# Copying gated tiles into planes of halves six products behind the gated product, with tiles of their own

## The chip, the core and the metric

The kernel runs on one core of a Trainium2 chip. Five engines work beside each other, each through its own queue of instructions in the order in which they were written: TensorE (PE, with PEld for the loading of weights), VectorE (DVE), ScalarE (ACT), GpSimd (POOL), and SyncE (SP), which here only issues DMAs. They wait for one another by semaphores. The metric is the device time of one execution in microseconds (us), lower being better, taken as the median of several runs. The profile is one execution recorded by the hardware profiler; its lines name engine, source line and tiles.

## The reference

A trunk of two layers over 256 tokens of width 1024, in float32. Each layer is a gated feed-forward stage, a mixer (attention) and another gated feed-forward stage, so there are four feed-forward stages, numbered 0, 2, 3 and 5 in the kernel (1 and 4 are the mixers):

```python
def swiglu(h, w_gate, w_up, w_down):
    return (jax.nn.silu(h @ w_gate) * (h @ w_up)) @ w_down

for layer in range(DEPTH):
    x = x + 0.5 * swiglu(rms_norm(x, ffn1_norm[layer]), ...)
    x = x + mixer(rms_norm(x, mix_norm[layer]))
    x = x + 0.5 * swiglu(rms_norm(x, ffn2_norm[layer]), ...)
return rms_norm(x, final_norm)
```

The hidden width of a feed-forward stage is 2816. The change touches only these stages: the product silu(gate) * up, called the gated product here, and its way to the down projection.

## The kernel before

**Split products.** Every float32 operand is split in two parts, hi (rounded to the format that PE takes) and lo (the rest). One product of a 128-deep slice is three matmuls (hi x hi, lo x hi, hi x lo; `mm`, lines 466 to 468). Weights come by DMA in tiles called raw (line 376, three buffers of up to 1 MB, issued by SP once a buffer is free), ACT makes hi (line 474) and DVE makes lo (line 477). Seven pairs of split tiles may be alive.

**Tokens and chunks.** The 256 tokens are two halves (tt = 0, 1) of 128 rows. A feed-forward stage runs over five chunks of 512 hidden columns and a mixed one of 256. A plain chunk takes gate for both halves (2 x 8 products), then up for both (2 x 8 products). Some chunks are done by a Strassen scheme instead (`seven_gates`), with 29 or 30 products and sums on DVE (lines 392 and 762 to 808). After the chunks come the down products, partly by Strassen pairs too, for which blocks of the gated tiles are summed (`quarters`, `sums_of`).

**The way of a gated tile.** ACT applies silu to the gate (line 667 or 785), DVE multiplies with up (`glu`, line 672, or line 789 in a Strassen chunk) and the result lies in a tile glu (ring of two). It must be transposed. This is done by DMA on 16-bit halves: ACT copies the tile into two planes, the low and the high halves (line 551), SP issues a DMA transpose of the planes back into the tile glu (line 553), and ACT copies the transposed halves together again into the tile of the planes (line 555). From there ACT and DVE make the parts g_h and g_l (lines 474 and 477), which the down products read. The tile of the planes has the tag silu, in a ring of three, shared with the results of silu and with the temporaries of the Strassen sums.

**What sets the order.** Each engine's queue has the order in which the program issues instructions. PE's order is written out by the loops. Everything else is done by generators (tasks): `mm` ends in `tick`, which counts one product and lets every task whose count has run out issue its next piece, and which also issues the next hi and lo parts when a rate says so. A `yield n` in a task puts its next piece n products later. So `GLU_WAIT` is the number of products between the issue of the gated product and that of the first copy, `TURN_WAIT[0]` that between the copy and the DMA transpose, and `TURN_WAIT[1]` that between the transpose and the second copy. These numbers set a place in the queues, not a time: an instruction waits in its queue until what it needs is there, and what stands behind it waits as well.

Of the kernel before, what the change touches and what calls it, by code (L numbers as in the profile page):

```python
# [18 lines left out]
P = 128  # L19
# [32 lines left out]

X_WAIT = 5
R_WAIT = 3
GLU_WAIT = 1
TURN_WAIT = [1, 8]
NAT_WAIT = 2
ROPE_WAIT = [3, 3]
KB_WAIT = {
# [143 lines left out]
class Trunk:  # L203
# [342 lines left out]

    def turned_over(self, m, w):

        two = self.t([P, 512], "silu", 3)
        planes, back = (t.bitcast(U16)[:, : 2 * w] for t in (two, m))  # L550
        self.nc.scalar.copy(planes.rearrange("p (h c) -> p h c", h=2), back.rearrange("p (c h) -> p h c", h=2))  # L551
        yield TURN_WAIT[0]
        self.nc.sync.dma_start_transpose(back.rearrange("p (j t) -> p j t", t=P), planes)
        yield TURN_WAIT[1]
        self.nc.scalar.copy(planes.rearrange("p (c h) -> p h c", h=2), back.rearrange("p (h c) -> p h c", h=2))  # L555
        yield 1
        return two
# [96 lines left out]
    def ffn(self):  # L654
# [96 lines left out]
        def seven_gates(f0, w, pairs7):  # L751

            while len(K) < 4:
                self.tick(False)
            self.rate = SEVEN_RATE[self.now.n]
            h, M, c = self.now.hT, {}, {}
            op = nc.vector.tensor_tensor

            def copy():
                yield 1  # L760
                c["m"] = self.t([P, 512], "glu", 2)
                nc.scalar.activation(c["m"], M["1"], AF.Copy)

            def common():

                yield 1
                while "m" not in c:
                    yield 1
                w = self.t([P, 512], "silu", 3)
                op(w, M["6"], c["m"], op=ALU.add)  # L770
                yield 1
                y = self.t([P, 512], "glu", 2)
                op(y, M["5"], w, op=ALU.subtract)
                yield 1
                nc.vector.scalar_tensor_tensor(w, M["7"], -1.0, w, op0=ALU.mult, op1=ALU.add)
                c["y"], c["w"] = y, w

            def first_gate():
                yield 1
                while "m" not in c:  # L780
                    yield 1
                s = self.t([P, 512], "silu", 3)
                op(s, M["00"], c["m"], op=ALU.add)
                yield 1
                nc.scalar.activation(s, s, AF.Silu, scale=self.now.r[0])
                c["s"] = s

            def up(tt, o, u, s):
                nc.vector.scalar_tensor_tensor(o, u, self.now.r[tt], s, op0=ALU.mult, op1=ALU.mult)
                self.spawn(transposed(tt, f0, w, o), GLU_WAIT)  # L790
                yield 1

            def rest():
                yield 1
                while "s" not in c or "w" not in c:
                    yield 1
                y, z, m = c["y"], c["w"], c["m"]
                op(y, M["01"], y, op=ALU.add)
                yield 1
                tasks.append(self.start(up(0, y, y, c["s"])))  # L800
                yield 1
                op(m, M["10"], z, op=ALU.add)
                yield 1
                nc.scalar.activation(m, m, AF.Silu, scale=self.now.r[1])
                op(z, M["5"], z, op=ALU.subtract)
                yield 1
                if "11" in M:
                    op(z, M["11"], z, op=ALU.add)
                    yield 1
                tasks.append(self.start(up(1, m, z, m)))  # L810

            def product(name, lh, piece, first, last):
                self.mm(M[name], lh, piece, first, last)

            n7 = KD // 2 - pairs7
            M.update((name, self.bank(tag)) for name, tag in [("00", "s"), ("01", "s"), ("10", "s")])
            if n7:
                M["11"] = self.bank("o")
            for q in range(KD // 2):
                k, first, last = 2 * q, q == n7, q == KD // 2 - 1  # L820
                if q < n7:
                    pieces = self.take(4)
                    for i in range(2):
                        for n, piece in enumerate(pieces[2 * i : 2 * i + 2]):
                            for tt in range(NT):
                                product(f"{tt}{n}", h[tt][k + i], piece, k + i == 0, tt == n == 1 and i == 1 and q + 1 == n7)
                    continue
                b11, b21, b22, t7, t5, t8, t6 = self.take(7)
                if first:
                    for task in tasks:  # L830
                        self.finish(task)
                    M.update((name, self.bank(tag)) for name, tag in [("1", "pj"), ("5", "pj"), ("7", "tp")])
                    M["6"] = self.bank("tp" if n7 else "o")
                j = q - (KD // 2 - most)
                product("1", h[0][k + 1], b11, first, last)
                if last:
                    self.start(copy())
                product("00", h[0][k], b21, q == 0, last)
                if last:
                    tasks.append(self.start(first_gate()))  # L840
                product("01", K[0][j], b22, q == 0, last)
                product("7", K[3][j], t7, first, last)
                product("5", K[2][j], t5, first, last)
                product("10", h[1][k], t8, q == 0, last)
                product("6", K[1][j], t6, first, last)
            self.start(common())
            tasks.append(self.start(rest()))

        f0 = 0
        self.spawn(x_sums())  # L850
        for ci, w in enumerate(FF_CHUNKS):
            if ci in sevens:
                seven_gates(f0, w, sevens[ci])
                f0 += w // P
                continue
            self.rate = (AHEAD_RATE if ci + 1 in sevens else RATE)[self.now.n]

            tags = ["pj", "s", "s", "pj"] if ci - 1 in sevens else ["s", "s", "pj", "pj"]
            G = self.take(KD)
            S = []  # L860
            if self.now.n + ci == 0:
                both = self.first_gates(G)
            for tt in range(NT):
                g = both[tt] if self.now.n + ci == 0 else self.project(self.ready(tt), G, tags[tt])
                S.append(self.t([P, 512], "silu", 3))
                self.start(silu(tt, w, g, S[tt]))
            U = self.take(KD)
            for tt in range(NT):
                u = self.project(self.now.hT[tt], U, tags[NT + tt])
                tasks.append(self.start(glu(tt, f0, w, u, S[tt])))  # L870
            f0 += w // P

        w, V = FF_MIXED, self.take(KD)
        for tt in range(NT):
            both = self.project(self.now.hT[tt], V, "s")
            s = self.t([P, 512], "silu", 3)
            self.start(silu(tt, w, both, s))
            tasks.append(self.start(glu(tt, f0, w, both[:, w:], s)))
        W = {}
# [46 lines left out]
        def combine():  # L926

            op = nc.vector.scalar_tensor_tensor
            x = lambda tt, i: self.x[tt][:, i * 512 : i * 512 + 512]
            more = lambda o, y: nc.vector.tensor_tensor(o, o, y, op=ALU.add)  # L930
            yield 1
            c = self.t([P, 512], "silu", 3)
            nc.scalar.activation(c, M["1"], AF.Copy, scale=0.5)
            op(x(0, 0), M["1"], 0.5, x(0, 0), op0=ALU.mult, op1=ALU.add)
            yield 1
            v = self.t([P, 512], "silu", 3)
            op(v, M["6"], 0.5, c, op0=ALU.mult, op1=ALU.add)
            yield 1
            w = self.t([P, 512], "glu", 2)
            op(w, M["7"], -0.5, v, op0=ALU.mult, op1=ALU.add)  # L940
            yield 1
            y = self.t([P, 512], "silu", 3)
            op(y, M["5"], 0.5, v, op0=ALU.mult, op1=ALU.subtract)
            yield 1
            more(x(0, 1), y)
            z = self.t([P, 512], "glu", 2)
            yield 1
            op(z, M["5"], 0.5, w, op0=ALU.mult, op1=ALU.subtract)
            yield 1
            more(x(1, 0), w)  # L950
            yield 1
            more(x(1, 1), z)
# [610 lines left out]
```

## Time and profile before

| | us |
|---|---|
| median of three runs | 1036.34 |
| the three runs | 1036.03, 1036.34, 1039.86 |
| the profiled execution | 1039.17 |
| its span, first to last instruction | 1037.4 |

The mean granted clock of TensorE over the span is 0.974 of full speed. A row of the page's second part shows it in 40 slices of the span (tenths of full speed, 9 being 90% or more):

```profile
PEclk9998999999999989999999998999999999999999
```

Rows of the timeline give the start and the length of an instruction in us, then engine, line, operation, tiles written and read, shapes, and in brackets how long the engine was idle before it and what it had waited for. Rows of the windows give a stretch, its length, the busy time of each engine in it with the number of its instructions, the granted clock, the DMA engines' share and GB/s. Rows of the waits give who waited for whom: us in total, times, and the longest.

### The profile page before, as it was taken

The numbers are of one execution on the slowest core, as the hardware profiler recorded it, in microseconds if no ns is written. First come the engines' busy times: TensorE is split into PE (matmuls) and PEld (weight loads), VectorE is DVE, ScalarE is ACT, GpSimd is POOL, SyncE is SP. The second block draws the span as 40 slices with busy tenths as digits, with TensorE's granted clock in tenths as the row PEclk, the third lists the DMA queues.
The fourth block names the chain that finished last, engine by engine and source line by source line (L and its number), as shares of the span: only waits on it lengthen the run. The fifth ranks groups of instructions, "written<-read, shape, count | busy, mean of one in ns | idle before, by whom it ended". The sixth has DMA issues, their size and how long they took to land.

```text
span 1037.4 us, 12414 instructions
## 1 busy us (share of the span) xinstructions
PE 957.1 (92%) x4399; PEld 764.5 (74%) x4399; DVE 792.6 (76%) x1228; ACT 681.5 (66%) x1091; POOL 92.6 (9%) x152
## 2 busy tenths in 40 slices
PE   9979999899998988899899888899999999789897
PEld 6757778777786766678787666688878888577676
DVE  6777658778877858669977774889777687765698
ACT  7665767477785566675666665666777676656653
POOL 1300000064410000000100000005230000000001
PEclk9998999999999989999999998999999999999999
DMA  8746665555245755556567565475534365466552
GB/s 297 246 134 211 194 195 202 203 137 108 82 124 158 236 147 189 167 188 249 168 181 236 146 194 180 140 269 160 166 123 137 117 209 179 150 204 183 172 206 79
DMA packets 129343, 183.16 MB, mean 177 GB/s; under 512 B 50688, under 2 KB 63744, under 8 KB 129280
## 3 DMA queue, kind: packets, MB, share of 16 engines
q1 hardware_dynamic: 128704, 181.58, 56.1%
q8 instruction: 34, 0.56, 0.2%
q10 hardware_dynamic: 576, 0.79, 0.2%
q14 instruction: 29, 0.24, 0.1%
HBM read 169.76 MB, written 1.05 MB: 165 GB/s over the span
## 4 chain that ended last, share of the span: by engine, by line
DVE 31%; PE 28%; ACT 18%; DMA 12%; issue 9%; SPq 0%; POOL 0%; ACTq 0%; POOLq 0%; DVEq 0%
DVE lo L477 12%; ACT hi L474 7%; DMA glu<-silu 7%; PE pj L466 5%; PE pj L468 4%; ACT silu L555 4%; PE pj L467 4%; DVE raw L392 3%; DVE two L392 2%; DVE slo L477 2%; PE s L467 2%; PE s L468 2%; PE s L466 2%; DMA raw<-in_ffn_w_up 2%; DVE g_l L477 2%
## 5 line engine op out<-in xcount | busy, mean ns | idle before, releaser
L477 DVE TENSOR_TENSOR lo<-raw,hi 128x1024 fp32r<-128x1024 f32 (+1 forms) x372 | 375.5, 1031 | 139.2 <-ACT hi L474 138.3
L474 ACT ACTIVATE hi<-raw 128x1024 fp32r<-128x1024 f32 (+1 forms) x372 | 316.3, 888 | 34.1 <-PE s L468 9.5
L467 PE MATMUL s<-lo,th 128*128 128x512 f32 x373 | 151.4, 406 | 18.8 <-DVE lo L477 18.8
L466 PE MATMUL s<-hi,th 128*128 128x512 f32 x373 | 150.3, 403 | 17.9 <-ACT hi L474 14.7
L468 PE MATMUL s<-hi,tl 128*128 128x512 f32 x373 | 149.0, 399 | 0.0
L466 PE MATMUL pj<-hi,th 128*128 128x512 f32 x367 | 148.6, 405 | 0.2 <-ACT hi L474 0.2
L467 PE MATMUL pj<-lo,th 128*128 128x512 f32 x367 | 145.3, 396 | 2.1 <-DVE lo L477 1.9
L468 PE MATMUL pj<-hi,tl 128*128 128x512 f32 x367 | 144.4, 393 | 0.0
L551 ACT COPY silu<-glu 128x1024 uint16<-128x1024 uint16 (+1 forms) x48 | 46.8, 975 | 112.9 <-DVE glu L672 79.9
L467 PEld LDWEIGHTS s<-lo,th 128*128 128x128 f32 x373 | 72.0, 193 | 40.7 <-DVE lo L477 26.5
L466 PEld LDWEIGHTS s<-hi,th 128*128 128x128 f32 x373 | 71.6, 192 | 37.7 <-ACT hi L474 19.7
L467 PEld LDWEIGHTS pj<-lo,th 128*128 128x128 f32 x367 | 70.2, 191 | 17.4 <-DVE lo L477 4.4
L468 PEld LDWEIGHTS s<-hi,tl 128*128 128x128 f32 x373 | 72.2, 193 | 14.5
L466 PEld LDWEIGHTS pj<-hi,th 128*128 128x128 f32 x367 | 70.3, 191 | 15.5 <-ACT hi L474 0.9
L468 PEld LDWEIGHTS pj<-hi,tl 128*128 128x128 f32 x367 | 69.9, 190 | 14.9
L486 POOL TENSOR_TENSOR rstd<-var,mhalf 128x1 f32<-128x1 f32 (+2 forms) x16 | 17.1, 1070 | 666.1 <-DVE var L484 469.8
L555 ACT COPY silu<-glu 128x1024 uint16<-128x1024 uint16 (+1 forms) x48 | 59.9, 1248 | 15.9 <-DMA glu<-silu 15.6
L474 ACT ACTIVATE shi<-two 128x1024 fp32r<-128x1024 f32 x30 | 31.7, 1057 | 38.1 <-DVE two L392 38.1
L466 PE MATMUL s<-hi,g_h 128*128 128x512 f32 (+1 forms) x131 | 53.0, 404 | 3.3 <-DVE glu L672 3.3
L477 DVE TENSOR_TENSOR g_l<-silu,g_h 128x512 fp32r<-128x512 f32 (+2 forms) x48 | 29.6, 618 | 29.9 <-ACT g_h L474 29.9
L468 PE MATMUL s<-hi,g_l 128*128 128x512 f32 (+1 forms) x131 | 52.4, 400 | 0.0
L467 PE MATMUL s<-lo,g_h 128*128 128x512 f32 (+1 forms) x131 | 52.3, 399 | 0.0
(483 smaller groups left out, 1698.4 us busy)
## 6 DMA issues: line engine op xcount, KB each, us to landing
raw<-in_ffn_w_down SPq DMA_DIRECT2D x44, 1024.0 KB, 5.2
raw<-in_ffn_w_up SPq DMA_DIRECT2D x28, 1024.0 KB, 5.2
raw<-in_ffn_w_gate SPq DMA_DIRECT2D x26, 1024.0 KB, 5.2
raw<-in_ffn_w_gate SPq DMA_DIRECT2D x35, 512.0 KB, 4.0
raw<-in_ffn_w_up SPq DMA_DIRECT2D x32, 512.0 KB, 5.0
raw<-in_odd_w_qkv SPq DMA_DIRECT2D x12, 1024.0 KB, 5.5
raw<-in_even_w_in SPq DMA_DIRECT2D x4, 1024.0 KB, 5.2
raw<-in_even_w_out SPq DMA_DIRECT2D x8, 512.0 KB, 5.9
```

Of the source, the lines that this page charges most:

```text
L392: add = lambda o, x, y: self.nc.vector.tensor_tensor(o, x, y, op=ALU.add)
L466: mm(ps, h, wh, start=first, stop=False)
L467: mm(ps, h, wl, start=False, stop=False)
L468: mm(ps, l, wh, start=False, stop=last)
L474: self.nc.scalar.activation(hi, src, AF.Copy)
L477: self.nc.vector.tensor_tensor(lo, src, hi.bitcast(F32), op=ALU.subtract)
L486: nc.gpsimd.tensor_tensor(r[:, :n], v[:, :n], self.mhalf[:, :n], op=ALU.pow)
L551: self.nc.scalar.copy(planes.rearrange("p (h c) -> p h c", h=2), back.rearrange("p (c h) -> p h c", h=2))
L555: self.nc.scalar.copy(planes.rearrange("p (c h) -> p h c", h=2), back.rearrange("p (h c) -> p h c", h=2))
```

## The change

Three things change in the feed-forward stages, and in nothing else. The first copy (line 551) is issued six products behind the gated product instead of one. The DMA transpose is issued two products behind the copy instead of one; the second copy stays eight products behind the transpose. And the planes have a tag of their own, turned, with two buffers, while the ring silu goes from three buffers to two.

```diff
-GLU_WAIT = 1
-TURN_WAIT = [1, 8]
+GLU_WAIT = 6
+TURN_WAIT = [2, 8]
...
     def turned_over(self, m, w):
 
-        two = self.t([P, 512], "silu", 3)
+        two = self.t([P, 512], "turned", 2)
         planes, back = (t.bitcast(U16)[:, : 2 * w] for t in (two, m))
...
-                S.append(self.t([P, 512], "silu", 3))
+                S.append(self.t([P, 512], "silu", 2))
```

The last pair of lines stands for seven more places in which the ring silu is asked for (in `seven_gates`, in the mixed chunk and in `combine`), with the same edit. Each instruction of the program stays; PE and POOL keep their order, and on ACT, DVE and SP some rows change places.

The first place is ACT's queue at the end of the first Strassen chunk of stage 0 and the start of the chunk behind it. glu_817 and glu_774 are the gated tiles of the two halves, hi are parts of the next weights. Before:

```order
L474 ACTIVATE hi_828<-raw_753 128x1024
L551 COPY silu_838<-glu_817 128x1024
L804 ACTIVATE glu_774<-glu_774,rstd_258 128x512
L474 ACTIVATE hi_850<-raw_772 128x1024
L551 COPY silu_863<-glu_774 128x1024
L667 ACTIVATE silu_858<-pj_807,rstd_213 128x512
L474 ACTIVATE hi_873<-raw_772 128x1024
L555 COPY silu_838<-glu_817 128x2x512
```

and now:

```order
L474 ACTIVATE hi_828<-raw_749 128x1024
L804 ACTIVATE glu_774<-glu_774,rstd_258 128x512
L474 ACTIVATE hi_847<-raw_772 128x1024
L667 ACTIVATE silu_855<-pj_807,rstd_213 128x512
L551 COPY turned_864<-glu_817 128x1024
L474 ACTIVATE hi_869<-raw_772 128x1024
L551 COPY turned_885<-glu_774 128x1024
L474 ACTIVATE hi_887<-raw_799 128x1024
L667 ACTIVATE silu_898<-s_856,rstd_258 128x512
L474 ACTIVATE hi_904<-raw_799 128x1024
L555 COPY turned_864<-glu_817 128x2x512
```

The two copies moved behind one hi part and the silu of the next chunk; the second half of raw_772 now stands ahead of the second copy, and two more hi parts and a silu ahead of the first second copy.

The second place is SP's queue at the end of stage 0's gate and up products. glu_1135 and glu_1181 are the two halves of the last plain chunk, the next one is of the mixed chunk. Before:

```order
L376 DMA raw_1149<-in_ffn_w_down 128x2x1024
L553 DMA_TRANSPOSE glu_1135<-silu_1140 128x8x128
L376 DMA raw_1172<-in_ffn_w_down 128x2x1024
L553 DMA_TRANSPOSE glu_1181<-silu_1190 128x8x128
L376 DMA raw_1236<-in_ffn_w_down 128x2x1024
L553 DMA_TRANSPOSE glu_1222<-silu_1227 128x4x128
```

and now:

```order
L376 DMA raw_1147<-in_ffn_w_down 128x2x1024
L376 DMA raw_1169<-in_ffn_w_down 128x2x1024
L553 DMA_TRANSPOSE glu_1135<-turned_1171 128x8x128
L553 DMA_TRANSPOSE glu_1181<-turned_1205 128x8x128
L376 DMA raw_1233<-in_ffn_w_down 128x2x1024
L376 DMA raw_1256<-in_ffn_w_down 128x2x1024
L553 DMA_TRANSPOSE glu_1218<-turned_1258 128x4x128
```

The first and the third transpose each moved behind one load of weights.

The third place is ACT's queue at the same time, up to the silu of the mixed chunk, whose glu frees the bank for the down products. Before:

```order
L551 COPY silu_1140<-glu_1135 128x1024
L474 ACTIVATE hi_1142<-raw_997 128x1024
L474 ACTIVATE hi_1155<-raw_1060 128x1024
L474 ACTIVATE hi_1165<-raw_1060 128x1024
L474 ACTIVATE hi_1183<-raw_1091 128x1024
L551 COPY silu_1190<-glu_1181 128x1024
L555 COPY silu_1140<-glu_1135 128x2x512
L474 ACTIVATE g_16_h_1200<-silu_1140 128x512
L667 ACTIVATE silu_1216<-s_1177,rstd_213 128x256
```

and now:

```order
L474 ACTIVATE hi_1162<-raw_1059 128x1024
L551 COPY turned_1171<-glu_1135 128x1024
L474 ACTIVATE hi_1183<-raw_1082 128x1024
L551 COPY turned_1205<-glu_1181 128x1024
L555 COPY turned_1171<-glu_1135 128x2x512
L667 ACTIVATE silu_1210<-s_1176,rstd_213 128x256
L474 ACTIVATE g_16_h_1223<-turned_1171 128x512
```

The first copy moved behind three hi parts; the second copy (L555) of the first half still stands directly ahead of the silu of the mixed chunk, and its g_h moved behind that.

More of the change, by code (lines that the diff above doesn't have):

```diff
@@ L768, in common @@
                     yield 1
-                w = self.t([P, 512], "silu", 3)
+                w = self.t([P, 512], "silu", 2)
                 op(w, M["6"], c["m"], op=ALU.add)
@@ L781, in first_gate @@
                     yield 1
-                s = self.t([P, 512], "silu", 3)
+                s = self.t([P, 512], "silu", 2)
                 op(s, M["00"], c["m"], op=ALU.add)
@@ L875, in ffn @@
             both = self.project(self.now.hT[tt], V, "s")
-            s = self.t([P, 512], "silu", 3)
+            s = self.t([P, 512], "silu", 2)
             self.start(silu(tt, w, both, s))
@@ L931, in combine @@
             yield 1
-            c = self.t([P, 512], "silu", 3)
+            c = self.t([P, 512], "silu", 2)
             nc.scalar.activation(c, M["1"], AF.Copy, scale=0.5)
@@ L935, in combine @@
             yield 1
-            v = self.t([P, 512], "silu", 3)
+            v = self.t([P, 512], "silu", 2)
             op(v, M["6"], 0.5, c, op0=ALU.mult, op1=ALU.add)
@@ L941, in combine @@
             yield 1
-            y = self.t([P, 512], "silu", 3)
+            y = self.t([P, 512], "silu", 2)
             op(y, M["5"], 0.5, v, op0=ALU.mult, op1=ALU.subtract)
```

## The prediction, made before the changed kernel ran

> **What bounds the kernel now.** I read the page first: how busy each engine is over the span.
>
> ```profile
> span 1037.4 us, 12414 instructions
> PE 957.1 (92%) x4399; PEld 764.5 (74%) x4399; DVE 792.6 (76%) x1228; ACT 681.5 (66%) x1091; POOL 92.6 (9%) x152
> ```
>
> PE is idle for 1037.4 - 957.1 = 80.3 us, so a change that moves no PE instruction can only win there, and in time that PE spends at a lower clock. Next the chain that ended last, by line:
>
> ```profile
> DVE lo L477 12%; ACT hi L474 7%; DMA glu<-silu 7%; PE pj L466 5%; PE pj L468 4%; ACT silu L555 4%; PE pj L467 4%; DVE raw L392 3%; DVE two L392 2%; DVE slo L477 2%; PE s L467 2%; PE s L468 2%; PE s L466 2%; DMA raw<-in_ffn_w_up 2%; DVE g_l L477 2%
> ```
>
> Splitting the weights (hi on ACT, lo on DVE) leads it, and the round trip of the gated tile (the DMA transpose glu<-silu and the copy behind it, L555) has 11%. Then the view of waits, all engines (us in total, times, longest):
>
> ```profile
> DVE lo L477 <- ACT hi L474: 138.3, 97, 3.5
> ACT silu L551 <- DVE glu L672: 79.9, 35, 5.8
> ACT silu L551 <- DVE glu L789: 32.9, 12, 4.8
> PE s L467 <- DVE lo L477: 18.8, 19, 2.2
> ACT silu L555 <- DMA glu<-silu: 15.6, 13, 2.5
> PE s L466 <- ACT hi L474: 14.7, 11, 4.0
> ACT silu L667 <- DVE g_l L477: 5.7, 4, 2.0
> ```
>
> The first copy of a gated tile (L551) makes ACT stand still for 79.9 + 32.9 = 112.8 us in 47 waits, 2.4 us each, because it is asked for one product after the gated product, and DVE has splits queued ahead of that. ACT works in the order of its queue, so the next hi parts stand behind the copy, DVE's lo parts behind those, and PE behind both. The last question is where PE's idle time lies: the view by windows over the four stretches that hold the gate and up products (length; busy us of PE, PEld, DVE, ACT, POOL; granted clock).
>
> ```profile
> 24.00:164.00 140.00, 129.31 (x540) 102.36 (x539) 98.11 (x118) 91.98 (x113) 9.29 (x22) 0.98 0.64 192
> 312.00:460.00 148.00, 130.10 (x528) 101.80 (x527) 105.13 (x127) 93.41 (x115) 0.00 (x0) 0.95 0.59 182
> 516.00:662.00 146.00, 131.48 (x541) 104.87 (x539) 103.44 (x131) 93.06 (x117) 0.00 (x0) 0.95 0.59 177
> 842.00:986.00 144.00, 130.68 (x541) 102.42 (x540) 99.96 (x126) 94.18 (x118) 0.00 (x0) 0.98 0.63 185
> ```
>
> PE idles 10.7 + 17.9 + 14.5 + 13.3 = 56.4 us there, and the clock takes 0.02 x 140 + 0.05 x 148 + 0.05 x 146 + 0.02 x 144 = 20.4 us more. These 77 us are all that this change can reach; attention, the down products and the edges of the span hold no such copy and I leave them as they are.
>
> **One place in full.** The timeline behind the first Strassen chunk of stage 0, ACT and then PE (start, length, in brackets the idle time ahead and what ended it):
>
> ```profile
> 90.81 1.05 ACT L551 COPY silu<-glu 128x1024 uint16<-128x1024 uint16 x1 [3.77 <-DVE glu L789]
> 93.17 1.04 ACT L474 ACTIVATE hi<-raw 128x1024 fp32r<-128x1024 f32 x1
> 96.23 1.05 ACT L551 COPY silu<-glu 128x1024 uint16<-128x1024 uint16 x1 [2.01 <-DVE glu L789]
> 97.76 1.04 ACT L474 ACTIVATE hi<-raw 128x1024 fp32r<-128x1024 f32 x1
> 98.86 0.50 PE L466 MATMUL s<-hi,th 128*128 128x512 f32 x1 [1.50 <-ACT hi L474]
> 101.81 0.63 PE L468 MATMUL s<-hi,tl 128*128 128x512 f32 x1
> 102.23 0.63 PE L466 MATMUL pj<-hi,th 128*128 128x512 f32 x1
> 104.10 0.40 PE L468 MATMUL pj<-hi,tl 128*128 128x512 f32 x1
> 104.33 0.39 PE L466 MATMUL pj<-hi,th 128*128 128x512 f32 x1
> ```
>
> ACT waits twice for a gated product; the hi part at 97.76 stands behind both, and PE waits for it until 98.86. Behind the wait, matmuls start 0.42 us apart instead of 0.23 us. In the new order of ACT, shown with the change, that hi part stands ahead of the second copy and has only the first, whose glu is long done, in front of it. From the same rows, a product of three matmuls takes 3 x 0.23 = 0.69 us, so five products are 3.4 us.
>
> **What the change gives, term by term.** No instruction is added or removed; 48 copies move five products (3.4 us) later, and what follows them six. A mean wait of 2.4 us fits into 3.4 us, the longest (5.8 us) doesn't. I sort the places where PE loses time behind such a copy into three kinds: the middle of Strassen chunks, the start of the chunk behind one, and plain chunks with the mixed one. Rows with a clock under 1 stand with each sum; 6 stretches make the second sum, 8 the third.
>
> ```profile
> 62.00:80.00 18.00, 12.48 (x42) 8.62 (x43) 13.98 (x19) 14.53 (x18) 0.00 (x0) 0.91 0.35 108
> 328.00:343.00 15.00, 9.94 (x33) 6.51 (x32) 12.28 (x15) 9.93 (x14) 0.00 (x0) 0.89 0.36 97
> 882.00:904.00 22.00, 15.49 (x52) 10.10 (x51) 16.94 (x22) 15.69 (x19) 0.00 (x0) 0.92 0.36 110
> sum 55.00, PE 37.91 PEld 25.23 DVE 43.19 ACT 40.15 POOL 0.00; mean PE 12.64 PEld 8.41 DVE 14.40 ACT 13.38 POOL 0.00
> 97.00:104.00 7.00, 4.74 (x13) 3.24 (x12) 3.05 (x3) 5.88 (x9) 0.00 (x0) 0.76 0.74 187
> 363.00:374.00 11.00, 7.34 (x21) 5.21 (x20) 5.85 (x7) 7.73 (x9) 0.00 (x0) 0.69 0.50 135
> 919.00:927.00 8.00, 5.10 (x15) 3.54 (x15) 4.62 (x6) 7.48 (x10) 0.00 (x0) 0.79 0.49 134
> sum 37.00, PE 23.82 PEld 15.85 DVE 19.54 ACT 32.05 POOL 0.00; mean PE 3.97 PEld 2.64 DVE 3.26 ACT 5.34 POOL 0.00
> 573.00:582.00 9.00, 5.89 (x20) 4.36 (x18) 6.05 (x11) 4.17 (x6) 0.00 (x0) 0.81 0.10 14
> 631.00:644.00 13.00, 8.26 (x23) 6.07 (x22) 7.31 (x10) 7.03 (x8) 0.00 (x0) 0.74 0.48 143
> sum 37.00, PE 24.84 PEld 17.02 DVE 24.70 ACT 26.17 POOL 0.85; mean PE 3.11 PEld 2.13 DVE 3.09 ACT 3.27 POOL 0.11
> ```
>
> - Inside Strassen chunks PE loses 55 - 37.9 = 17.1 us idle and 0.09 x 18 + 0.11 x 15 + 0.08 x 22 = 5.0 us of clock. DVE is busy 43.2 of the 55 us and would be next: without any wait of its own it still needs 43.2, so the gain ends at 11.8. Bounds 0 and 11.8; I take **8**, since ACT's waits are the main ones that DVE has here, but quarters and g_h still have to pass.
> - Behind a Strassen chunk PE loses 13.2 us idle and 1.7 + 3.4 + 1.7 = 6.8 us of clock, 20.0 in all. DVE has slack (19.5 of 37), so bounds are 0 and 20. The place above is the model, and there nothing remains; I take four fifths, **16**.
> - In plain chunks PE loses 12.2 us and 1.7 + 3.4 = 5.1 us of clock, 17.3 in all. Here the second copy and its DMA fall nearer to the silu of the next product. Bounds 0 and 17.3; I take three fifths, **10**.
>
> The own tiles are part of this: the silu of the next chunk (L667) waits 5.7 us for a g_l that reads a turned tile in the same ring of three, and with a ring of its own that goes. The fewer silu buffers cost nothing by the order: a chunk uses two, both read by glu before the next chunk asks, and combine asks for a third when its first has been read.
>
> The clock term deserves a word. The rows show half speed (0.42 us a matmul) behind waits of 1.50 us, and the granted clock of 0.76 and 0.69 in such stretches. The Trainium skill, "TensorE: Matmul & The Clock Gate", Part 1, has the clock halve after an idle window of about 3.4 us. By that alone waits this short would leave the clock alone, and the 16.9 us that the rows show (5.0 + 6.8 + 5.1) would not hang on them; here the trace differs, and I keep them in the sum.
>
> **What it costs.** Three queues are moved past something.
>
> ```profile
> L551 ACT COPY silu<-glu x48: 619/1046/1048, 26.1 to 980.6; 128x1024 uint16<-128x1024 uint16 x40, 128x512 uint16<-128x512 uint16 x8
> DMA to landing us min/median/max: 2.4/3.2/6.7
> SPq L376 <- DVE lo L477: 435.8, 106, 14.0
> ```
>
> ACT: copy, transpose and second copy now stand 2 + 8 = 10 products apart, 6.9 us. A copy of 1.05 us and a landing of 3.2 us (median) fit; with the longest, 6.7 us, L555 waits 0.9 us, and more where SP is late. An ACT that comes early meets this wait more often. Bounds: all 15.6 us of L555's waits vanish, or each of 48 waits the longest 2.5 us, 120 us. I take the near row doubled, 15.6 us more on ACT. Over the three kinds PE lost 17.1 + 13.2 + 12.2 + 16.9 = 59.4 us to ACT's 112.8 + 15.6 + 5.7 = 134.1 us of such waits, 0.44 each; so 15.6 x 0.44 = **7 us** lost. SP: some transposes now stand behind a weight load, which waits for a lo part, 4.1 us in the mean; in return lo parts come earlier, and I put no more on it. DVE: a gated tile lives six products longer in a ring of two, so the mixed chunk's glu meets L555 of the chunk before; that is the slow rival below.
>
> Sum: 8 + 16 + 10 - 7 = 27 us. The profiled span of 1037.4 us lies in an execution of 1039.17 us, and the median is 1036.34: the saving is taken from the median, 1036.3 - 27 = **1009 us**. With all upper bounds and no new wait it would be 1036.3 - 11.8 - 20 - 17.3 = 987.
>
> **Rivals.** *The wait moves to L555.* For: 15.6 us are there already, and landings of 6.7 us are as long as the distance. Against: the copies start sooner after their glu, and SP waits less for them. If 20 of the 34 us come back there, 1036.3 - 14 = 1022.
>
> *Slower: the ring of two gated tiles holds DVE at the mixed chunk.* Its glu needs the buffer that L555 of the chunk before frees, and that stood six products (4.1 us) ahead and now stands level. Place: the start of the down products.
>
> ```profile
> 143.00 1.36 ACT L555 COPY silu<-glu 128x1024 uint16<-128x1024 uint16 x1 [2.46 <-DMA glu<-silu]
> 145.66 0.48 DVE L672 SCALAR_TENSOR_TENSOR glu<-s,rstd,silu 128x256 f32<-128x256 f32 x1
> 146.19 0.50 PE L466 MATMUL s<-hi,g_h 128*128 128x512 f32 x1 [0.70 <-DVE glu L672]
> ```
>
> PE waits for this glu already, and splits stand behind it on DVE. If both halves of the four stages come 5 us late, 8 x 5 = 40 us are lost against the 27: 1049. It decides from 27 / 8 = 3.4 us. Against: on ACT the second copy stands ahead of the silu that this glu needs anyway, and copies start right behind their glu.
>
> *No change*: hi parts that no longer stand behind copies meet PE's own release of weight buffers, and the waits stay under other names: 1036. Against: PE did wait for those hi parts.
>
> *The clock stays* though the waits go, because the half-speed stretches hang on something else: 34 x 16.9 / 59.4 = 10 us less, 1019. Against: each such stretch above begins behind a wait. This is also what the rule of the Trainium skill's page on the clock gate would make of waits this short.
>
> **Chances.** Forecast 0.65, wait at L555 0.17, clock stays 0.05, no change 0.07, slower 0.06. Faster by over 0.5% (5.2 us, about what a measurement here can tell from no change) takes the first three, 0.87. The range from 990 (near all the upper bounds) to 1029 (past the wait at L555) leaves out the last two and some of the forecast's edge.
>
> **What would show it.** Right: L551's waits fall from 112.8 to under 40 us, L667's wait for g_l is gone, PE's idle time falls from 80 to about 60 us, and the mean granted clock rises from 0.974. L555's wait at about 31 us confirms the cost; 60 us or more means the first rival. Wrong: PE waiting for glu at the start of the down products over 3 us per stage, or PE's waits for lo as long as now.

## The result, and the profile after

| | before | after |
|---|---|---|
| median in us (4 runs each; of before the three shown and a fourth) | 1037.33 | 1029.45 |
| all runs | 1036.03 to 1039.86 | 1028.81 to 1029.61 |
| the profiled execution | 1039.17 | 1029.36 |
| its span | 1037.4 | 1027.6 |

The ratio is 0.992, with a 95% interval from 0.9898 to 0.9941: the change is worth 0.8%, 7.9 us. The forecast was 27 us (1009, range 990 to 1029).

The busy times on the page of the changed kernel, in the form that the prediction began with:

```profile
span 1027.6 us, 12420 instructions
PE 959.0 (93%) x4399; PEld 769.4 (75%) x4399; DVE 792.7 (77%) x1228; ACT 679.3 (66%) x1091; POOL 87.5 (9%) x152
```

PE is idle for 1027.6 - 959.0 = 68.6 us instead of 80.3. The same page's chain by line, and its rows on the two copies (out and in, times | busy us, mean ns | idle time ahead and what ended it):

```profile
DMA glu<-turned 11%; DVE lo L477 10%; PE pj L466 7%; PE pj L467 7%; PE pj L468 7%; ACT hi L474 5%; PE s L467 5%; PE s L468 5%; PE s L466 5%; ACT turned L555 3%; DVE slo L477 2%; DVE raw L392 2%; DVE two L392 2%; PE o L1035 2%; ACT turned L551 1%
...
L555 ACT COPY turned<-glu 128x1024 uint16<-128x1024 uint16 (+1 forms) x48 | 60.0, 1250 | 75.8 <-DMA glu<-turned 75.8
...
L551 ACT COPY turned<-glu 128x1024 uint16<-128x1024 uint16 (+1 forms) x48 | 46.3, 964 | 15.4 <-DVE glu L672 13.1
```

The first copy waits 15.4 us where it waited 112.8. The second copy (L555) waits 75.8 us where it waited 15.6, and the DMA transpose now leads the chain. The view of waits of the changed kernel (total, times, longest):

```profile
DVE lo L477 <- ACT hi L474: 95.8, 81, 8.3
ACT turned L555 <- DMA glu<-turned: 75.8, 31, 4.9
DVE glu L672 <- ACT silu L667: 26.5, 4, 6.9
PE s L467 <- DVE lo L477: 12.6, 15, 2.0
PE s L466 <- DVE glu L672: 8.9, 4, 3.2
ACT glu L804 <- DVE glu L802: 24.3, 6, 5.7
```

and one line of the same view of the kernel before, for comparison:

```profile
ACT glu L804 <- DVE glu L802: 1.3, 2, 0.7
```

Where 47 waits of 2.4 us stood at the first copy, 31 waits of 2.4 us now stand at the other end of the same round trip. Another part of the old waits did not vanish either: L804, the silu of the second half in a Strassen chunk, stood behind a copy that waited and, as the order shown with the change has it, now stands ahead of both copies. It waits 24.3 us for DVE where it waited 1.3, so 23 of the 97.4 us that left L551 are still spent there. The transposes themselves, by the view of line 553 in the changed kernel:

```profile
DMA to landing us min/median/max: 3.0/5.6/7.4
```

The median landing went from 3.2 to 5.6 us.

**Where it was gained and where it was given back.** PE's order is the same in both kernels, so the n-th matmul of lines 466 to 468 in one trace is the n-th in the other (3714 in each). For the three kinds of places of the prediction I took the first matmul at each end of its stretches in the trace of before, and the time between the same two matmuls in every other trace. "Elsewhere" is the rest of the four stretches of gate and up products, "outside" what lies outside of these four, and "all" goes from the first such matmul to the last. This is worked out from the traces, in us against before:

```
                               inside  behind  plain   sum  elsewhere  outside  all
predicted                         -8     -16    -10    -34      +7         0    -27
changed kernel                 -15.0   -18.6   -3.7  -37.4   +31.9      -4.3   -9.8
own tiles alone                 -0.3    +0.6  -11.1  -10.7    +2.1      -1.5  -10.2
copies moved, [1, 9]           -15.9   -18.9   -9.7  -44.5   +34.3      -7.3  -17.5
second copy at 12, three glu   -17.9   -18.3  -18.2  -54.3    +8.1      +0.4  -45.8
transposes by ACT              -18.3   -18.3  -18.6  -55.3   +15.5      -7.7  -47.6
same, three glu                -19.6   -17.8  -18.2  -55.6   +19.1      -7.8  -44.2
same, three glu, copy at 12    -17.4   -18.7  -18.7  -54.7    +0.3      +7.4  -47.1
own tiles, second copy at 12    -9.7    +2.4  -16.1  -23.4    -2.7      -4.6  -30.8
own tiles, transposes by ACT    +2.1    +5.8  -11.4   -3.4    +0.4      +2.5   -0.6
```

The lower rows are the experiments below; each row is one execution, and two of them lie well above their medians, the last by 4.7 us and "same, three glu" by 2.9. The gain came, and a little more of it than forecast (37.4 against 34). The cost came to 31.9 us instead of 7. The stretches were chosen because PE lost time there in before, so some of the gain could be chance alone; the row with own tiles alone, in which nothing but the tiles differs, shows none of that inside and behind the Strassen chunks (-0.3 and +0.6).

**The place of the prediction.** The timeline of the changed kernel behind the first Strassen chunk of stage 0, ACT:

```profile
89.75 0.72 ACT L804 ACTIVATE glu<-glu,rstd 128x512 f32<-128x512 f32 x1 [5.71 <-DVE glu L802]
90.38 1.04 ACT L474 ACTIVATE hi<-raw 128x1024 fp32r<-128x1024 f32 x1
...
91.89 1.03 ACT L551 COPY turned<-glu 128x1024 uint16<-128x1024 uint16 x1
92.83 1.06 ACT L474 ACTIVATE hi<-raw 128x1024 fp32r<-128x1024 f32 x1
93.79 1.03 ACT L551 COPY turned<-glu 128x1024 uint16<-128x1024 uint16 x1
94.73 1.06 ACT L474 ACTIVATE hi<-raw 128x1024 fp32r<-128x1024 f32 x1
```

Neither copy waits, and the hi part between them starts when the first is done; before, ACT waited 3.77 and 2.01 us at the copies here. ACT still stands for 5.71 us, at L804, but now all of it ahead of the hi parts and none between them, and PE gains behind the Strassen chunks as foreseen (-18.6 us in the table). The next plain chunk of the same stage, in the timelines of ACT, of PE and of SP:

```profile
115.67 1.05 ACT L551 COPY turned<-glu 128x1024 uint16<-128x1024 uint16 x1 [0.90 <-DVE glu L672]
121.38 1.33 ACT L555 COPY turned<-glu 128x1024 uint16<-128x1024 uint16 x1 [4.67 <-DMA glu<-turned]
...
123.98 2.94 ACT L474 ACTIVATE hi<-raw 128x1024 fp32r<-128x1024 f32 x3
```

```profile
119.88 0.39 PE L468 MATMUL pj<-hi,tl 128*128 128x512 f32 x1
125.07 0.80 PE L466 MATMUL pj<-hi,th 128*128 128x512 f32 x1 [4.80 <-ACT hi L474]
```

```profile
115.36 0.51 SPq L376 DMA_DIRECT2D raw<-in_ffn_w_up  x1
115.96 4.40 SPq L553 DMA_TRANSPOSE glu<-turned  x2
```

SP issues a weight load, then two transposes. ACT has nothing to do ahead of the second copy, stands for 4.67 us, and the hi parts for which PE waits are queued behind it: PE idles 4.80 us, and its next matmuls take 0.80 us. Against before, PE loses 7.8 us in the 12 us from 119.8 on.

### The profile page after: what moved, and what is told of

It reads as the page before. It is cut to its first block, busy times and chain, and to the rows that moved or that the text cites. A ratio compares the mean times of both kernels' runs of the same rounds, so it can differ in the third digit from the quotient of the medians.

```text
span 1027.6 us, 12420 instructions
## 1 busy us (share of the span) xinstructions
PE 959.0 (93%) x4399; PEld 769.4 (75%) x4399; DVE 792.7 (77%) x1228; ACT 679.3 (66%) x1091; POOL 87.5 (9%) x152
## 4 chain that ended last, share of the span: by engine, by line
PE 44%; DVE 21%; DMA 14%; ACT 14%; issue 5%; SPq 1%; POOL 0%; ACTq 0%; POOLq 0%; DVEq 0%
DMA glu<-turned 11%; DVE lo L477 10%; PE pj L466 7%; PE pj L467 7%; PE pj L468 7%; ACT hi L474 5%; PE s L467 5%; PE s L468 5%; PE s L466 5%; ACT turned L555 3%; DVE slo L477 2%; DVE raw L392 2%; DVE two L392 2%; PE o L1035 2%; ACT turned L551 1%
## 5 line engine op out<-in xcount | busy, mean ns | idle before, releaser
L555 ACT COPY turned<-glu 128x1024 uint16<-128x1024 uint16 (+1 forms) x48 | 60.0, 1250 | 75.8 <-DMA glu<-turned 75.8
L466 PEld LDWEIGHTS pj<-hi,th 128*128 128x128 f32 x367 | 71.2, 194 | 23.5 <-ACT hi L474 7.6
L486 POOL TENSOR_TENSOR rstd<-var,mhalf 128x1 f32<-128x1 f32 (+2 forms) x16 | 17.1, 1070 | 668.5 <-ACT th L507 361.9
L477 DVE TENSOR_TENSOR g_l<-turned,g_h 128x512 fp32r<-128x512 f32 (+2 forms) x48 | 29.5, 614 | 38.4 <-ACT g_h L474 38.4
L551 ACT COPY turned<-glu 128x1024 uint16<-128x1024 uint16 (+1 forms) x48 | 46.3, 964 | 15.4 <-DVE glu L672 13.1
```

The source lines that it names most:

```text
L466: mm(ps, h, wh, start=first, stop=False)
L477: self.nc.vector.tensor_tensor(lo, src, hi.bitcast(F32), op=ALU.subtract)
L486: nc.gpsimd.tensor_tensor(r[:, :n], v[:, :n], self.mhalf[:, :n], op=ALU.pow)
```

## The experiments

Each is the kernel named, with the edit shown or told; "Measured" gives the median, its ratio to the kernel before measured beside it (1036.8 to 1037.8), and the 95% interval of the ratio.

**Own tiles alone** (e2_tiles). The changed kernel with the order of before:

```diff
-GLU_WAIT = 6
-TURN_WAIT = [2, 8]
+GLU_WAIT = 1
+TURN_WAIT = [1, 8]
```

> Own tiles alone: the tag turned with two buffers and two silu buffers, but the first copy again one product behind the gated product and the transpose one behind the copy (GLU_WAIT 1, TURN_WAIT [1, 8]). Theory (the gain of 8 us comes from moving the copies, and what is missing is eaten by waits for transposes): only the 5.7 us of waits of L667 for g_l go, L551 still waits about 110 us, time 1031 to 1036. Rival (the tiles bring the whole gain and the moved copies nothing): 1029.

Measured: 1030.26 us, ratio 0.9937 (0.9921 to 0.9954). Its waits:

```profile
ACT turned L551 <- DVE glu L672: 79.9, 35, 6.0
ACT turned L551 <- DVE glu L789: 35.1, 12, 4.8
ACT turned L555 <- DMA glu<-turned: 14.2, 14, 2.3
```

One buffer more (two rings of two in the place of one of three) brings as much as the whole change, with L551's waits as long as ever. L667's wait for a g_l, 5.7 us before, is gone, and by the table the gain lies in the plain chunks. The rival of this expectation held. So the moved copies are worth nothing on balance in the changed kernel (1030.3 against 1029.5), and the question became what eats their gain.

**Copies moved, the issue one product behind the copy** (e3_copy). The changed kernel with

```diff
-TURN_WAIT = [2, 8]
+TURN_WAIT = [1, 9]
```

> As after, but the transpose is issued one product behind its copy and the second copy nine behind the transpose (TURN_WAIT [1, 9]): all three ACT instructions stay where they are and only the transposes move up on SP. Theory (transposes land late because a weight load stands ahead of them): L555's wait falls from 75.8 us to 45 to 60 and the time to 1022 to 1027. Rival (the sharing of the DMA engines alone sets the landing): the landing stays at 5.6 us in the median, and the wait falls by the one product at most, 31 x 0.69 = 21 us, time 1025 to 1029.

Measured: 1022.3 us, 0.9859 (0.9837 to 0.9881), with L555 waiting 71.2 us. The time lies in the range of the theory, but its sign, 45 to 60 us at L555, did not come: the landing (median 5.5 us) and the waits at L555 hardly change. In the mean a transpose starts 1.27 us behind the end of its copy, against 1.39 us in the changed kernel, so why this place in the queue is worth 7 us stays open.

**The second copy farther out** (e1_later). The changed kernel with

```diff
-TURN_WAIT = [2, 8]
+TURN_WAIT = [2, 12]
...
-            m = self.t([P, 512], "glu", 2)
+            m = self.t([P, 512], "glu", 3)
```

(the last pair stands for all five places of that ring).

> As after, but the second copy twelve products behind the transpose instead of eight (TURN_WAIT [2, 12]), with three buffers for gated tiles so that nothing new waits for them. Theory (what is missing is lost to L555's wait for the DMA): its wait of 75.8 us falls under 25, PE's waits for hi and shi behind it (22 us) mostly go, time 1008 to 1018. Rival (hi parts are held by PE's release of weight buffers or by DVE, and the waits only change names): L555's wait falls all the same, time 1026 to 1031.

Measured: 994.15 us, 0.9597 (0.9574 to 0.962); L555's wait:

```profile
ACT turned L555 <- DMA glu<-turned: 36.9, 19, 3.7
```

With four more products between the transpose and its second copy, L555's wait halves and 35 us come off the changed kernel. That is more than either branch allowed, though the wait fell by less than the theory said (under 25 us).

**The same with two gated tiles** (e7_later2), to price the slow rival:

> TURN_WAIT [2, 12] with the ring of two gated tiles as in after: the run before without its third buffer. If the longer distance between transpose and second copy brings the 35 us, the time stays within 5 us of 994. If the third buffer of gated tiles does it (DVE's glu of the mixed chunk waits for L555 in a ring of two), the time is 1020 or more.

Measured: 1005.79 us, 0.9695 (0.9675 to 0.9715). Its waits:

```profile
DVE glu L672 <- ACT turned L555: 51.8, 13, 6.9
ACT turned L555 <- DMA glu<-turned: 40.3, 21, 3.5
```

The time lies between the two branches. The mechanism of the slow rival is real: DVE waits for L555 to free a gated tile, and the third tile is worth 12 us here. But it begins only at the longer distance: in the changed kernel DVE has no such wait.

**Three gated tiles at the distance of the change** (e8_glu3):

> After with three buffers for gated tiles and nothing else changed. By the slow rival of the prediction (the mixed chunk's glu waits for L555 in a ring of two), DVE's 26.5 us of waits and PE's 8.9 us for that glu go and the time falls by 8 to 15 us, 1014 to 1021. By the theory that L555's wait for the DMA is all, the glu waits for the silu that stands behind L555 on ACT, not for a buffer, and the time stays at 1027 to 1031.

Measured: 1028.29 us, 0.9913 (0.9894 to 0.9933), 1 us from the changed kernel: no effect that can be told from none. In the changed kernel the glu of the mixed chunk waits for its silu, which stands behind L555 (26.5 us above), and not for a buffer.

**One ring of four** (e5_ring4) instead of two rings of two, all other things as changed:

```diff
-        two = self.t([P, 512], "turned", 2)
+        two = self.t([P, 512], "silu", 4)
```

(and 4 for 2 at the seven other places of the ring silu).

> The moved copies (GLU_WAIT 6, TURN_WAIT [2, 8]) with the same two buffers for planes and two for silu, but in one shared ring of four instead of tags of their own. If the separate tags are what brings after's 8 us, this is 5 to 8 us slower than after, 1034 to 1038. If only the number of buffers matters, it is after's time within 3 us.

Measured: 1028.54 us, 0.9914 (0.9897 to 0.993). The separate tag is worth nothing here, which leaves the fourth buffer as what the own tiles brought. One ring of four with the copies at their old place, and the moved copies with the old ring of three, are in no run.

**Transposes issued by ACT** (e6_actq). The changed kernel with

```diff
-        self.nc.sync.dma_start_transpose(back.rearrange("p (j t) -> p j t", t=P), planes)
+        self.nc.scalar.dma_start_transpose(back.rearrange("p (j t) -> p j t", t=P), planes)
```

> As after, but the transposes are issued by ACT on its own DMA queue right behind the other work there, no longer behind weight loads in SP's queue. If the landing time is set by what stands ahead in SP's queue, it falls from 5.6 us in the median to about 3; if it is set by the DMA engines that both share, it stays over 5. ACT pays the issue (1.2 to 1.6 us each, 48 times, some 65 us of its 348 us idle), so the time may go either way: 1022 to 1040.

Measured: 991.38 us, 0.9559 (0.9539 to 0.9578). The view of line 553 and its waits:

```profile
DMA to landing us min/median/max: 3.0/4.2/11.4
```

```profile
ACT turned L555 <- DMA glu<-turned: 27.3, 11, 7.3
```

The timeline of ACT at the plain chunk that was shown above:

```profile
112.14 1.03 ACT L551 COPY turned<-glu 128x1024 uint16<-128x1024 uint16 x1
113.07 1.35 ACT L555 COPY turned<-glu 128x1024 uint16<-128x1024 uint16 x1
113.19 1.25 ACTq L553 DMA_TRANSPOSE glu<-turned  x1
...
115.91 2.95 ACT L474 ACTIVATE hi<-raw 128x1024 fp32r<-128x1024 f32 x3
118.75 1.36 ACT L555 COPY turned<-glu 128x1024 uint16<-128x1024 uint16 x1
```

No row waits: the second copy of the first half finds its planes at 113.07, one instruction behind the first copy of the other half. The order of ACT's copies and parts is that of the change; only the queue that starts the transposes differs, and 38 us come off, where 1022 us at best was expected. The landing came out between the two branches. Both halves of the way to it got shorter: in the mean a transpose starts 0.49 us behind the end of its copy (1.39 in the changed kernel), and it lands 4.4 us later (5.4). The landing is still longer beside a weight load, 4.69 us for 38 of the 48 against 3.50 for the others, so leaving SP's queue does not end the sharing.

**Own tiles and transposes by ACT, copies not moved** (e9_tiles_actq):

> Own tiles with the old places (GLU_WAIT 1, TURN_WAIT [1, 8]) and the transposes issued by ACT. Its distance to 991.4 us is what moving the copies brings when the transposes no longer stand behind weight loads. The prediction put that at 27 us and its 34 us without new waits: 1018 to 1026. If taking the transposes off SP is worth the 38 us by itself, this is 991 to 1000.

Measured: 1033.2 us, 0.9965 (0.9951 to 0.9978), with L551 waiting 110.8 us and L555 5.5. Both branches fell. With the copies at their old place the queue brings nothing (3 us longer than own tiles alone). The issue stands one product behind the copy here, a place that costs much with the copies moved (e14_act19 below); ACT waits only 4.1 us for it in this run, but the copies at their old place with the issue two products behind are in no run.

**Own tiles, second copy at 12, copies not moved** (e12_dist) (GLU_WAIT = 1, TURN_WAIT = [1, 12], three gated tiles):

> Own tiles and three buffers for gated tiles with the copies at their old place (GLU_WAIT 1), but the second copy twelve products behind the transpose (TURN_WAIT [1, 12]). If the longer distance is worth its 24 us by itself, 1004 to 1012. If it is worth something only where the moved copies made L555 wait (14 us of its waits are left here, against 75.8 in after), L551 goes on waiting over 100 us and the time is 1026 to 1032.

Measured: 1008.49 us, 0.9711 (0.9695 to 0.9727), in the first branch: the distance is worth 22 us without the moved copies. Its waits:

```profile
ACT turned L551 <- DVE glu L672: 67.9, 28, 5.9
ACT turned L551 <- DVE glu L789: 33.5, 12, 4.8
ACT turned L555 <- DMA glu<-turned: 10.1, 7, 2.5
```

L551 waits nearly as long as in before (101.4 us), L555 had little to lose, and still it takes 22 us less than with own tiles alone. In ACT's queue most of the second copies, with the g_h and quarters behind them, stand one or two hi parts later. PE's waits for hi are no shorter for it, 10.7 us in both traces; those for glu (L672) fell from 7.8 to 3.4 us, for shi from 6.1 to 2.1 and for slo from 6.2 to 4.2. So L555's wait for the landing is not all that a late second copy saves, and what the rest is stays open. The third gated tile differs from own tiles alone too, but in the trace of own tiles alone DVE never waits for a gated tile to come free.

**Both remedies** (e10_best) (transposes by ACT, three gated tiles, TURN_WAIT = [1, 11]):

> Both remedies together: transposes on ACT's queue, three buffers for gated tiles, TURN_WAIT [1, 11]. If what is left of L555's wait (27.3 us) still costs PE, 975 to 986. If the two remedies take away the same thing, 987 to 995.

Measured: 1019.43 us, 0.9823 (0.9805 to 0.9841), 28 us longer than the changed kernel with the queue alone, and outside both branches. This edit moves the issue too, from two products behind the copy to one; the next three runs take it apart.

**The queue with three gated tiles at [2, 8]** (e11_actq3):

> The transposes on ACT's queue as in the run that gave 991.4, with three buffers for gated tiles, places as in after. If a third buffer matters only where L555 is late or far, as it did by 12 us with twelve products and not at all with eight, this is 988 to 993.

Measured: 992.08 us, 0.9553 (0.9528 to 0.9577): the third tile is nothing here.

**The queue with the issue one product behind the copy** (e14_act19) (transposes by ACT, TURN_WAIT = [1, 9], two gated tiles):

> Changed kernel with the transposes issued by ACT and TURN_WAIT [1, 9] (issue one product behind the copy, the second copy at the same place as in e6_actq). Theory: an issue directly behind its copy makes ACT stand until the copy has drained, and that is what made e10_best slow: ACT's hi parts wait for the issue for more than 12 us, and the time is 1003 to 1020 us. Rival: the distance of 11 was at fault in e10_best, and the place of the issue is worth no more than on SP (changed kernel against its [1, 9]: 7 us, to the other side): 983 to 995 us.

Measured: 1012.26 us, 0.9746 (0.9719 to 0.9773). The timeline of ACT at the same plain chunk:

```profile
112.72 1.03 ACT L551 COPY turned<-glu 128x1024 uint16<-128x1024 uint16 x1
113.78 1.25 ACTq L553 DMA_TRANSPOSE glu<-turned  x1
115.12 1.06 ACT L474 ACTIVATE hi<-raw 128x1024 fp32r<-128x1024 f32 x1 [1.38 <-issue]
116.09 1.03 ACT L551 COPY turned<-glu 128x1024 uint16<-128x1024 uint16 x1
117.15 1.25 ACTq L553 DMA_TRANSPOSE glu<-turned  x1
118.44 1.35 ACT L555 COPY turned<-glu 128x1024 uint16<-128x1024 uint16 x1 [1.32 <-issue]
```

The theory held. The issue stands directly behind its copy and ahead of the next hi part, and ACT stands for it twice (29 us in all at hi and L555, against 5 us at [2, 8]). One product of distance is worth 21 us on this queue; on SP the same step brought 7 us the other way. This run also prices the moved copies with the issue left one product behind: 1033.2 - 1012.3 = 21 us by ACT's queue, and 1030.3 - 1022.3 = 8 us by SP's.

**The queue with the second copy at 12** (e13_act12) (transposes by ACT, three gated tiles, TURN_WAIT = [2, 12]):

> Changed kernel with the transposes issued by ACT, a ring of three gated tiles and TURN_WAIT [2, 12]: beside the changed kernel with three gated tiles (1028), the same at [2, 12] on SP (994) and at [2, 8] on ACT (992) it completes a square. Theory: distance and queue cure the same trouble, the second copy that waits for a late landing, and what the one leaves the other can take only in part: L555's wait below 20 us and 975 to 992 us. Rival: a second copy that stands far behind its transpose holds the two planes tiles longer than they can be held, and the next copy or a quarter waits for them (as in e10_best, 1019): 1005 us or more. The two would gain fully in sum only at 958, which neither expects.

Measured: 991.94 us, 0.9559 (0.9529 to 0.9588), with L555 waiting 5.2 us, at the edge of the theory's range. With the runs above it makes a square of three gated tiles:

| | second copy at 8 | at 12 |
|---|---|---|
| transposes by SP | 1028.3 | 994.2 |
| transposes by ACT | 992.1 | 991.9 |

Each remedy brings 34 to 36 us, both together no more. That alone does not show that they cure one and the same thing. By the table, with the transposes on ACT's queue the step from 8 to 12 still gains in the four stretches (54.4 us off there, against 39.8 and 36.5 in the two rows at 8) and gives 15 back outside of them (+7.4 against -7.7 and -7.8). A wait of the kind that the rival named is there too: over the span L551 waits 17.1 us for a g_l that reads a tile of planes (16.7 in e1_later, 2.2 in the changed kernel). No run has three tiles of planes, so whether this is what costs the 15 us is not shown. The distance as such isn't at fault in e10_best, since 12 products go with 992 us here; e14_act19 puts 21 of its 28 us down to the place of the issue, and 7 us stay open.

## Why the prediction was wrong in size

- **The first copies' waits.** Right: 112.8 to 15.4 us (under 40 was said), and L667's wait for g_l is gone, though 23 us of the waits moved to L804, which the prediction did not see; the gain came all the same. The gain behind the Strassen chunks was 18.6 us (16 said, model place 0 left), inside them 15.0 (8 said). The bound of 11.8 there was wrong: it held DVE to the 43.2 us of work that those stretches contained in before, yet the same products now take 39.2 us with DVE busy for 32.5, so part of that work left the stretch together with the moved parts.
- **Plain chunks.** 10 us were said, of which the own tiles were "part". The tiles alone gave 11.1, and moving the copies gave 7.4 of it back here. Where the landing is no trouble, the same places gain 18. Mixing two edits with different effects into one term hid both.
- **The step that failed is "What it costs".** It took L555's 15.6 us of waits, doubled them to about 31, and priced the new half at 0.44: 7 us. Measured: 75.8 us of L555 waits, 60.2 more than before, and 31.9 us lost elsewhere in the stages instead of 7. The new wait was mis-sized by a factor of four. The ratio of the two, 31.9 to 60.2 or 0.53, is near the 0.44 that was used, but this is luck in part: in e1_later 35 us came off with 38.9 us of that wait, in e12_dist 22 us with 4.1. The wait was mis-sized because the median landing of before, 3.2 us, was used for an order in which it no longer holds. The order shown with the change had the transposes behind weight loads in SP's queue, and the step said "I put no more on it". By the traces of before, the 36 of 48 transposes issued while a weight load was still on its way landed after 4.72 us in the mean, the others after 2.94; now 46 are of the first kind, at 5.47 us. The issue too came later, 1.39 us behind the copy's end in the mean instead of 0.87. The second copy stands 8 products, 8 x 0.69 = 5.5 us, behind the issue, for a landing whose median is now 5.6. That it is this wait that ate the gain is what e1_later and e6_actq show, which leave the copies moved, take most of it away and lose only 8.1 and 15.5 us elsewhere.
- **The rival "The wait moves to L555"** is what happened. Its sign in the profile was set at 60 us, and 75.8 came; its price, 20 of 34 us given back, was too small: 31.9 of 37.4 were.
- **The clock.** The granted clock was to rise from 0.974. It did not: the profiled execution has 0.966, the three others 0.973, 0.975 and 0.975. PE waits less often and a little longer (53 waits, at most 4.80 us, against 68, at most 3.98), and matmuls behind the longest take 0.80 us. The two others of 1027.8 us span lie within 0.2 us of the profiled one, so 0.007 to 0.009 x 1027.6 = 7 to 9 us of clock were lost without any time lost. I read this so that part of the slow matmuls lies where PE would have waited anyway; then idle time and lost clock can't be added as the prediction did. No run isolates it. Matmuls of 0.80 us behind a wait of 4.80 us agree with the rule of the Trainium skill, "TensorE: Matmul & The Clock Gate", Part 1 (an idle window of about 3.4 us); those behind 1.50 us, in before, still don't.
- **The slow rival** did not come in the changed kernel (PE waits 8.9 us for the mixed glu, 2.2 a stage, 3 was the mark), and shows at 12 products with two gated tiles.
- **No change** fell: the interval of the ratio ends at 0.9941, short of 1. But what moving the copies adds to the own tiles did come close to it.

What stays open: why the second copy at 12 helps by 22 us when the first copies still wait, what both remedies lose outside the stretches, and why single transposes on ACT's queue take up to 11 to 13 us. All the best versions end at 991 to 994 us with PE busy for 95%.

The shortest is the changed kernel with the transposes issued by ACT: 991.38 us against 1029.45. The two others at 992 us can't be told from it.

## What to carry to other kernels

When a copy that feeds a DMA is moved in a queue, follow the whole round trip: the wait for the producer that vanishes can come back at the consumer of the landing, unless the distance from the issue covers the landing as it is in the new order, with what now stands ahead of the DMA in its queue. Keep small transfers that an engine waits for out of the queue that starts the large loads, but don't put the issue directly behind its producer on the engine that is already short of time. To see where a change gained and gave back, align two traces by an engine whose order is unchanged; sums of waits over the whole span can't show it.

## What the runs showed of the hardware

- A DMA transpose of 128x1024 16-bit halves issued by SP landed after 3.1 us with no weight load on its way (mean of 10 in before) and after 4.8 us with one (30 in before), 5.6 us in the changed kernel (38); issued by ACT beside loads that SP issues, after 4.7 us (31).
- Two transposes issued by SP one behind the other took 4.40 us of its queue, 1.50 and 2.78 each, where one alone takes 1.2 us.
- Spans of 1027.6 and 1027.8 us of the same kernel came with mean granted clocks of 0.966, 0.973 and 0.975.
- With the issue of a transpose on ACT's queue directly behind the copy that it needs, the instruction behind the issue stood for 1.38 and 1.32 us (e14_act19).
